# The last norm of a hybrid decoder step: sums by the constant matrix, statistics per token column, a 128-row correction operand, two blocks of 128 tokens

## The chip, the cores and the metric

The kernel runs on one core of a Trainium2 chip. The metric is the device time of one execution in microseconds (us), taken as the median of the runs; lower is better.

## The reference

The reference computes one inference step of a four-layer decoder for 1024 prompt tokens and 8 sample tokens, with a width of 2048. Two layers mix by pooling, two by windowed attention, and each layer ends in a norm over the width. Only the last norm matters here. For each token it is

```python
def layer_norm(x, g, b):
    mu = jnp.mean(xf, axis=-1, keepdims=True)
    var = jnp.mean(jnp.square(xf - mu), axis=-1, keepdims=True)
    return (xf - mu) * lax.rsqrt(var + LN_EPS) * g + b
```

applied to `ALPHA * x + sublayer(x)`, where the sublayer ends in a 2048 by 2048 product with `w_out_b`. The outputs `y_prompt` and `y_sample` are these normalised rows.

## The kernel before, in words

The tokens are worked in two chunks: chunk 0 has 512 tokens, chunk 1 has 520 (512 of the prompt and the 8 samples). Activations lie with the width across the 128 partitions: 16 groups of 128 channels, handled as 8 pairs p = 0 to 7, each a tile of 128 x 2 x T. All large products go as f32 split into a high and a low part, three passes each (lines 643, 644 and 645), and by a seven-product scheme over half chunks of 260 columns. `ACT` casts the high part of each weight block (L476) and `DVE` subtracts to get the low part (L491), some blocks ahead of the product. The order of the instructions of PE, DVE and ACT is that of the source: a helper, `in_order`, ties each instruction to the one before it on its engine. The queue of SP (DMA issue) and that of POOL have no such tie.

The change lies in `phase_end`, which runs the last three pairs (5, 6 and 7, called x, y and z there) of the last output product of chunk 1, and with them the norm of that chunk. A table `steps` says which small jobs go behind which of the 21 products of these three pairs (`TAIL`). The 520 columns have two halves: `Bh` (columns 260 to 519), whose statistics are made while products still run, and `A` (columns 0 to 259), whose statistics can only be made at the end. `less`, `rest`, `square` and `add` build the pre-norm value and the running sums of values and of squares. For half `Bh`, `sums` multiplies the running sums by a constant 128x128 matrix J with all elements 1/2048 (L1292), so that each of the 128 partitions gets the mean of each token; `stats` turns these into mean and reciprocal deviation on 128x260 tiles (L1299 to L1301 and the helper `rstd`, L859 to L862); `affine1` (DVE, L1310 and L1311) and `affine2` (ACT, L1318) apply them to a pair, and L1319 stores it.

Half `A` goes another way. `scale` (ACT, L1330) multiplies each pair by its gain. `turn` (L1413) transposes blocks of 128 tokens on PE, so that tokens come to lie across partitions, four channel groups to one PSUM bank of 128x512. There are three token blocks: 128, 128 and 4. `columns` (L1364) makes the sums of each token by 24 f32 products (two instructions each) that stream one column of J past a block of values, which gives one sum per partition. `moments` works on 128x3 tiles (L1374 to L1393), `lay` transposes the results into 6 rows (L1400, L1404), and `last_rows` (L1422) adds minus mean times gain and deviation times bias to each bank by one product with those 6 rows against 6 rows of gains and biases. `evict` multiplies the bank by the reciprocal deviation on its way to SBUF, on ACT for even banks (L1438), on DVE for odd ones (L1435), and each two banks are stored as 512 KB (L1436). The 6 rows of gains and biases are prepared by `rows0`, `rows1` and `rows2`: load, split, store to a scratch tensor in DRAM (L1344), and 12 small loads of one row each (L1351).

After the last product of the loop the source gives, in this order: the square and scale of the last piece, `affine1` of pair 1, the transposes of block 0 but for pair 7, `columns`, `affine1` of pair 2, the other transposes, `affine2` of pairs 1 and 2, `moments`, `affine1` of pair 3, `lay`, `last_rows`, the evictions of block 0, and then blocks 1 and 2 with the affine steps of pairs 3 and 4 between them.

PSUM banks come from rings: `psD` (3 banks), `psW` (4 banks) and `psO` (1 bank). SBUF slots (`mem.full`, `mem.half`) come from a list of 53, the one longest free first.

Of the kernel before, what the change touches and what calls it, by code (L numbers as in the profile page):

```python
# [16 lines left out]
P = 128  # L17
# [164 lines left out]
class Kern:  # L182
    def __init__(self, ctx, tc, io):
# [13 lines left out]
        self.gbs = one.tile([32, 2 * P], F32R, name="gbs")  # L197
        self.hcol = one.tile([P, 6], F32R, name="hcol")
        self.rows = one.tile([8, THM], F32R, name="rows")
# [1045 lines left out]
    def phase_end(self, c, xs, x_in, pre, acc, gc, bc, out):  # L1245
# [16 lines left out]
        BLK = (0, P), (P, 2 * P), (2 * P, TH)  # L1262
# [62 lines left out]
        def scale(p, js=(0, 1), away=False):  # L1325
            if p not in gx:
                gx[p] = self.pair_view(self.mem.full(), T) if away else tv(p)
            for j in js:
                m = gc + 2 * p + j
                nc.scalar.activation(gx[p][:, j, A], tv(p)[:, j, A], AF.Copy, scale=self.prm[:, m : m + 1])  # L1330

        def rows0():

            s = self.mem.half()
            raw, hi, lo = s.a[:32, :P], self.gbs[:32, :P], self.gbs[:32, P : 2 * P]
            nc.sync.dma_start(raw, io["gb"])
            box["f"] = s, raw, hi, lo

        def rows1():
            s, raw, hi, lo = box["f"]  # L1340
            nc.scalar.copy(hi, raw)
            nc.vector.tensor_sub(lo, raw, hi.bitcast(F32))
            s.free()
            nc.sync.dma_start(self.gbd[:], self.gbs[:32].bitcast(F32))  # L1344

        def rows2():
            for u in range(2):
                g = box["g", u] = self.mem.full()
                for k, (w, i) in enumerate(((0, 0), (0, 1), (0, 0), (1, 0), (1, 1), (1, 0))):
                    r = 16 * w + 8 * u  # L1350
                    nc.sync.dma_start(  # L1351
                        g.a[k : k + 1, :1024].rearrange("p (a b) -> p a b", a=8),
# [3 lines left out]
        def columns():  # L1356

            ps = box["c"] = self.psO()
            w = SPLIT[-1]
            for i, (a, z) in enumerate(((av, tv(w)), (qv, self.pair_view(q[w], T)))):  # L1360
                for b, (lo, hi) in enumerate(BLK):
                    srcs = [v[:, j, lo:hi] for v in (a, z) for j in range(2)]
                    for k, v in enumerate(srcs):
                        nc.tensor.matmul(  # L1364
                            ps[: hi - lo, 3 * i + b : 3 * i + b + 1], v, J[:, :1], start=k == 0, stop=k == 3
                        )

        def moments():

            ps = box["c"]  # L1370
            S = self.mem.half().a
            col = lambda i: S[:, 3 * i : 3 * i + 3]
            box["C"] = C = S[:, 32:50].rearrange("p (b k i) -> p b k i", b=3, k=2)
            nc.vector.memset(S[:, :6], 1.0)  # L1374
            full = ps[:, :6].rearrange("p (i b) -> p i b", i=2)
            to = S[:, :6].rearrange("p (i b) -> p i b", i=2)
            nc.vector.tensor_copy(to[:, :, :2], full[:, :, :2])
            e = BLK[2][1] - BLK[2][0]
            nc.vector.tensor_copy(to[:e, :, 2:], full[:e, :, 2:])
            m, v, qq, r, nm, sd = (col(i) for i in range(6))  # L1380
            box["r"] = r
            nc.vector.tensor_mul(qq, m, m)
            nc.vector.scalar_tensor_tensor(v, v, EPS, qq, op0=ALU.add, op1=ALU.subtract)
            nc.vector.tensor_scalar(nm, m, -1.0, None, op0=ALU.mult)
            self.rstd(v, r, qq)
            nc.vector.tensor_mul(sd, v, r)
            hi = self.hcol[:]
            nc.scalar.copy(hi, S[:, 12:18])
            h3 = hi.bitcast(F32).rearrange("p (k b) -> p b k", k=2)
            x3 = S[:, 12:18].rearrange("p (k b) -> p b k", k=2)  # L1390
            nc.vector.tensor_copy(C[:, :, :, 0], h3)
            nc.vector.tensor_copy(C[:, :, :, 1], h3)
            nc.vector.tensor_sub(C[:, :, :, 2], x3, h3)  # L1393

        def lay():

            ps = box["c"]
            for b, (lo, hi) in enumerate(BLK):
                n = hi - lo
                nc.tensor.transpose(  # L1400
                    ps[:6, P + lo : P + hi], box["C"][:n, b].rearrange("p k i -> p (k i)"),
                    self.cst[:n, K_ID : K_ID + n],
                )
            nc.scalar.copy(self.rows[:6, :TH], ps[:6, P : P + TH])  # L1404

        def turn(b, ps):
            lo, hi = BLK[b]
            for p in ps:
                for j in range(2):
                    i = 2 * p + j  # L1410
                    if i % 4 == 0 and (b, i // 4) not in X:
                        X[b, i // 4] = self.psW() if b != 1 or i >= 12 else self.psD()
                    nc.tensor.matmul(  # L1413
                        X[b, i // 4][: hi - lo, (i % 4) * P : (i % 4 + 1) * P], gx[p][:, j, lo:hi],
                        self.cst[:, K_ID : K_ID + P], is_transpose=True, start=i % 4 == 0, stop=False,
                        skip_group_check=True,
# [820 lines left out]
```

## Time and profile before

| | |
|---|---|
| median of 3 runs | 2376.43 us (2375.75 to 2378.41) |
| the profiled execution, its own time | 2374.82 us |
| its span, first to last instruction | 2373.1 us |
| busy in the span: DVE, ACT, POOL | 81%, 56%, 8% |
| mean granted TensorE clock | 0.996 |
| DMA traffic in the span | 669.20 MB, 282 GB/s |

The times in the timeline views are microseconds from the start of the span. A row of a timeline gives the start, the duration, the engine, the line of the kernel, the operation, the tile written and the tiles read, and in brackets the idle time of the engine just before with what ended it. PE is the matmul stream, PEld the weight loads that run beside it. DMA-issuing instructions stand under SPq. The last product of the loop ends about 26 us ahead of the end of the span, and everything that the change touches behind the loop lies in these 26 us.

### The profile page before, as it was taken

Reading aid. Unit: us, or ns where it says so; the run is one execution under the profiler, and the core shown is the slowest. Engines: PE = TensorE matmul, PEld = TensorE weight load, DVE = VectorE, ACT = ScalarE, POOL = GpSimd, SP = SyncE. Lnnn points to the kernel's source line nnn. Section 1 sums busy time; section 2 is a strip of 40 time slices with the busy share of each in tenths; the row PEclk is TensorE's granted clock in tenths of the full one; section 3 lists DMA queues with packets and bytes.
Section 4 is the critical chain, followed back from the end, with each engine's and each line's share of the span. In section 5 each row is a group of like instructions: output and inputs, shape, how many; then the busy total and the mean of one; then the engine's idle time right before and its main releaser. Section 6 shows DMA issues by size and latency. Waiting matters only on the chain. (4 is left out here: it accounts for less than half of the span.)

```text
span 2373.1 us, 46646 instructions
## 1 busy us (share of the span) xinstructions
PE 2342.9 (99%) x18497; PEld 2227.8 (94%) x18497; DVE 1913.2 (81%) x2372; ACT 1338.0 (56%) x2419; POOL 195.4 (8%) x369
## 2 busy tenths in 40 slices
PE   8999999999999999999999999999999999999999
PEld 6899999999999999998878899999999999999998
DVE  8787998776878868958987888887776768888786
ACT  4444446444446447644555656675666667546555
POOL 0111110010000000001111111100000000000000
PEclk9999999999999999999999999999999999999998
DMA  8668889889889988989888776788776668699784
GB/s 293 213 248 299 279 287 360 311 301 318 288 308 333 320 274 323 330 302 330 308 318 301 253 235 218 266 277 280 234 245 218 222 191 298 228 369 365 266 306 163
DMA packets 251932, 669.20 MB, mean 282 GB/s; under 512 B 25624, under 2 KB 106424, under 8 KB 251712
## 3 DMA queue, kind: packets, MB, share of 16 engines
q1 hardware_dynamic: 206240, 501.14, 62.9%
q0 software_dynamic: 45472, 165.07, 17.9%
q8 instruction: 145, 2.38, 0.4%
q14 instruction: 75, 0.61, 0.1%
HBM read 471.01 MB, written 185.59 MB: 277 GB/s over the span
## 5 line engine op out<-in xcount | busy, mean ns | idle before, releaser
L643 PE MATMUL pD<-m,m 128*128 128x260 f32 (+1 forms) x4752 | 1348.5, 284 | 10.1 <-ACT pD L584 4.5
L645 PE MATMUL pD<-m,m 128*128 128x260 f32 (+1 forms) x4752 | 1340.2, 282 | 3.1 <-DVE m L491 3.1
L644 PE MATMUL pD<-m,m 128*128 128x260 f32 (+1 forms) x4752 | 1339.5, 282 | 0.0
L643 PEld LDWEIGHTS pD<-m,m 128*128 128x128 f32 x4752 | 895.4, 188 | 22.3 <-issue 10.1
L645 PEld LDWEIGHTS pD<-m,m 128*128 128x128 f32 x4752 | 896.0, 189 | 4.5 <-DVE m L491 4.3
L491 DVE TENSOR_TENSOR m<-m,m 128x1024 fp32r<-128x1024 f32 x674 | 814.0, 1218 | 103.4 <-ACT m L476 62.0
L644 PEld LDWEIGHTS pD<-m,m 128*128 128x128 f32 x4752 | 895.6, 188 | 1.7 <-issue 1.4
L476 ACT CAST m<-m 128x1024 fp32r<-128x1024 f32 x674 | 701.4, 1048 | 303.2 <-DVE m L334 72.3
L671 PE MATMUL pD<-m,m 128*128 128x512 f32 x448 | 179.7, 401 | 8.1 <-ACT m L754 8.1
L672 PE MATMUL pD<-m,m 128*128 128x512 f32 x448 | 177.0, 395 | 1.2 <-DVE m L763 1.2
L673 PE MATMUL pD<-m,m 128*128 128x512 f32 x448 | 176.9, 395 | 0.0
L763 DVE TENSOR_TENSOR m<-m,m 128x1024 fp32r<-128x1024 f32 (+1 forms) x120 | 146.7, 1224 | 7.5 <-ACT m L754 6.0
L616 ACT COPY m<-pD 128x260 f32<-128x260 f32 (+1 forms) x83 | 31.1, 374 | 195.3 <-PE pD L645 194.9
L754 ACT CAST m<-m 128x1024 fp32r<-128x1024 f32 (+1 forms) x120 | 125.8, 1053 | 13.4 <-PE pD L672 5.2
L671 PEld LDWEIGHTS pD<-m,m 128*128 128x128 f32 x448 | 84.5, 189 | 30.1 <-ACT m L754 8.3
L334 DVE TENSOR_TENSOR m<-m,m 128x1024 f32<-128x1024 f32 x88 | 107.5, 1222 | 4.9 <-DMA m<-in_wia 2.4
L672 PEld LDWEIGHTS pD<-m,m 128*128 128x128 f32 x448 | 84.6, 189 | 21.0 <-DVE m L763 2.2
L604 DVE TENSOR_TENSOR m<-pD,m 128x260 f32<-128x260 f32 (+1 forms) x86 | 36.4, 424 | 83.7 <-PE pD L645 83.4
L673 PEld LDWEIGHTS pD<-m,m 128*128 128x128 f32 x448 | 84.5, 189 | 19.8
L1706 ACT ACTIVATE m<-m,sm 128x128 f32<-128x128 f32 x256 | 99.2, 390 | 0.0
L1027 PE MATMUL pD<-m,m 128*128 128x260 f32 (+1 forms) x528 | 91.5, 323 | 0.0
L1027 PEld LDWEIGHTS pD<-m,m 128*128 128x128 f32 x528 | 79.5, 188 | 8.2
(224 smaller groups left out, 2128.7 us busy)
## 6 DMA issues: line engine op xcount, KB each, us to landing
m<-in_wia SPq DMA_DIRECT2D x124, 512.0 KB
m<-in_wib SPq DMA_DIRECT2D x120, 512.0 KB
swia<-m POOLq DMA_DIRECT2D x64, 512.0 KB, 4.8
m<-swia SPq DMA_DIRECT2D x64, 512.0 KB
m<-swoa SPq DMA_DIRECT2D x64, 512.0 KB
swib<-m POOLq DMA_DIRECT2D x64, 512.0 KB, 5.3
m<-swib SPq DMA_DIRECT2D x64, 512.0 KB
m<-swob SPq DMA_DIRECT2D x56, 512.0 KB
```

What stands on the lines that cost most here:

```text
L334: self.nc.vector.tensor_add(s[out].a[:, :1024], s[x].a[:, :1024], s[y].a[:, :1024])
L476: self.nc.scalar.copy(hi.r[:, :1024], self.stream[self.cast].src().a[:, :1024])
L491: self.nc.vector.tensor_sub(lo.r[:, :1024], s.src().a[:, :1024], hi.a[:, :1024])
L643: nc.tensor.matmul(ps[:, :TH], wh[:, s], h, start=new and k == 0, stop=False, skip_group_check=on)
L644: nc.tensor.matmul(ps[:, :TH], wh[:, s], l, start=False, stop=False, skip_group_check=on)
L645: nc.tensor.matmul(ps[:, :TH], wl[:, s], h, start=False, stop=k == 7, skip_group_check=on)
L671: nc.tensor.matmul(ps[:], wh[:, s], h, start=par == 0 and k == 0, stop=False)
L672: nc.tensor.matmul(ps[:], wh[:, s], l, start=False, stop=False)
L673: nc.tensor.matmul(ps[:], wl[:, s], h, start=False, stop=par == 1 and k == 7)
L754: self.nc.scalar.copy(h.r[:, :n], s.a[:, :n])
L763: self.nc.vector.tensor_sub(l.r[:, :n], s.a[:, :n], h.a[:, :n])
L1027: nc.tensor.matmul(ps[:, : cs.stop - cs.start], ws[:, s], d[:, cs], start=f0 and k == 0, stop=l0 and k == 3,)
```

## The change

The sums of half `A` are made as those of half `Bh` are: by products with J into two banks (`sums_a`, 8 products of 128x260, in three portions). The statistics are made on 128x260 tiles. The correction operand gets 128 rows: minus the mean lies in rows 0 to 63, the deviation in rows 64 to 127, with the high part in rows 0 to 31 and 64 to 95 and the low part in the others; of the gains and biases only rows 0, 1, 32, 64, 65 and 96 are loaded, and the rest is zero, set by two 128x1024 memsets on POOL. The reciprocal deviation of a token, which the evictions need per partition, is had by transposing the statistics tile (`factors`, `factors2`). There are two token blocks of 128. The last 4 tokens of half `A` go apart: `spare` copies their 4 columns of each pair on POOL into a small tile ahead of `scale`, `scale` runs on 256 columns in place of 260, and `last_four` normalises them with four DVE operations on 128x64 and stores them to an output of their own. The scale of pair 6 moves from the step of the last product to behind it, the first 8 transposes move ahead of the sums, and the banks are taken from other rings.

```diff
-        self.gbs = one.tile([32, 2 * P], F32R, name="gbs")
-        self.hcol = one.tile([P, 6], F32R, name="hcol")
-        self.rows = one.tile([8, THM], F32R, name="rows")
...
-        BLK = (0, P), (P, 2 * P), (2 * P, TH)
+        A2 = slice(0, 2 * P)
+        four = self.small(NK * 4, 1)
+        f3 = four[:].rearrange("p (k t) -> p k t", k=NK)
...
-                nc.scalar.activation(gx[p][:, j, A], tv(p)[:, j, A], AF.Copy, scale=self.prm[:, m : m + 1])
+                nc.scalar.activation(gx[p][:, j, A2], tv(p)[:, j, A2], AF.Copy, scale=self.prm[:, m : m + 1])
+
+        def spare(p):
+            nc.gpsimd.tensor_copy(f3[:, 2 * p : 2 * p + 2, :], tv(p)[:, :, 2 * P : TH])
...
         def rows1():
-            s, raw, hi, lo = box["f"]
-            nc.scalar.copy(hi, raw)
-            nc.vector.tensor_sub(lo, raw, hi.bitcast(F32))
+            s, h = box["f"]
+            nc.scalar.copy(h.r[:32, :P], s.a[:32, :P])
+            nc.vector.tensor_sub(h.r[:32, P : 2 * P], s.a[:32, :P], h.a[:32, :P])
             s.free()
-            nc.sync.dma_start(self.gbd[:], self.gbs[:32].bitcast(F32))
+            nc.sync.dma_start(self.gbd[:], h.a[:32, : 2 * P])
+            h.free(True)
+            for u in range(2):
+                box["g", u] = self.mem.full()
+                nc.gpsimd.memset(box["g", u].a[:, :1024], 0.0)
 
         def rows2():
             for u in range(2):
-                g = box["g", u] = self.mem.full()
-                for k, (w, i) in enumerate(((0, 0), (0, 1), (0, 0), (1, 0), (1, 1), (1, 0))):
+                for k, w, i in ((0, 0, 0), (1, 0, 1), (32, 0, 0), (64, 1, 0), (65, 1, 1), (96, 1, 0)):
...
+        def sums_a(js):
+
+            z = SPLIT[-1]
+            if not js:
+                R[0] = self.psW(), self.psW()
+            for ps, a, w in zip(R[0], (av, qv), (tv(z), self.pair_view(q[z], T))):
+                for j in js or (0, 1):
                     nc.tensor.matmul(
+                        ps[:, :TH], J, (w if js else a)[:, j, A], start=not js and j == 0, stop=js == (1,),
                         skip_group_check=True,
                     )
 
+        def moments():
+
+            mb, vb = R[0]
+            w, h, S = self.mem.full(), self.mem.full(), [self.mem.half() for _ in range(4)]
+            m, v, qq, r = (t.a[:, :TH] for t in S)
+            X, M = w.a[:, : 2 * P], h.r[:, : 2 * P]
+            box["m"], box["r"], box["M"] = m, r, M
+            hi, lo = slice(0, 64), slice(64, P)
+            back32 = lambda k: nc.vector.tensor_sub(
+                M[k : k + 32], X[k : k + 32], h.a[k : k + 32, : 2 * P]
+            )
+            nc.scalar.copy(m, mb[:, :TH])
+            nc.vector.tensor_mul(qq, m, m)
+            nc.scalar.mul(X[hi], mb[hi, A2], -1.0)
+            nc.vector.scalar_tensor_tensor(v, vb[:, :TH], EPS, qq, op0=ALU.add, op1=ALU.subtract)
+            nc.scalar.activation(r, v, AF.Abs_reciprocal_sqrt)
+            nc.scalar.copy(M[hi], X[hi])
+            nc.vector.tensor_mul(qq, r, r)
+            nc.vector.scalar_tensor_tensor(qq, qq, -0.5, v, op0=ALU.mult, op1=ALU.mult)
+            nc.vector.scalar_tensor_tensor(r, qq, 1.5, r, op0=ALU.add, op1=ALU.mult)
+            nc.vector.tensor_mul(X[lo], v[lo, A2], r[lo, A2])
+            nc.scalar.copy(M[lo], X[lo])
+            back32(32)
+            back32(96)
+
+        def factors():
+
+            ps = box["c"]
+            for b in range(2):
+                nc.tensor.transpose(
+                    ps[:, b * P : (b + 1) * P], box["r"][:, b * P : (b + 1) * P], self.cst[:, K_ID : K_ID + P]
+                )
+
+        def factors2():
+            rc = box["rc"] = self.small(2, 1)
+            nc.scalar.copy(rc[:], box["c"][:, : 2 * P].rearrange("p (b t) -> p b t", b=2)[:, :, 0])
...
         def last_rows(b, ks):
-            lo, hi = BLK[b]
             for k in ks:
                 nc.tensor.matmul(
-                    X[b, k][: hi - lo], self.rows[:6, lo:hi], box["g", k // 2].r[:6, (k % 2) * 512 : (k % 2 + 1) * 512],
+                    X[b, k][:], box["M"][:, b * P : (b + 1) * P],
+                    box["g", k // 2].r[:, (k % 2) * 512 : (k % 2 + 1) * 512],
                     start=False, stop=True, skip_group_check=True,
                 )
...
+        def last_four():
+
+            wide = lambda a: a[:, None, 2 * P : TH].to_broadcast([P, NK, 4])
+            over = lambda i: self.prm[:, i : i + NK, None].to_broadcast([P, NK, 4])
+            nc.vector.tensor_sub(f3, f3, wide(box["m"]))
+            nc.vector.tensor_mul(f3, f3, wide(box["r"]))
+            nc.vector.tensor_mul(f3, f3, over(gc))
+            nc.vector.tensor_add(f3, f3, over(bc))
+            nc.sync.dma_start(io["y1c"], f3)
...
         square(z, A, 1)
+        spare(y)
+        spare(z)
         scale(z, (1,))
+        scale(y)
         affine1(1, Bh)
-        turn(0, range(z))
-        columns()
+        affine2(1, Bh)
+        X[0, 0], X[0, 1] = self.psD(), self.psD()
+        turn(0, 0, 8)
+        sums_a(())
+        sums_a((0,))
+        sums_a((1,))
+        X[0, 2], X[0, 3] = self.psW(), self.psW()
+        turn(0, 8, 16)
+        X[1, 0], X[1, 1] = self.psO(), self.psD()
+        turn(1, 0, 8)
         affine1(2, Bh)
-        turn(0, (z,))
-        turn(1, range(6))
-        affine2(1, Bh)
+        moments()
+        X[1, 2] = self.psW()
+        turn(1, 8, 12)
         affine2(2, Bh)
-        moments()
+        box["c"] = self.psW()
+        factors()
+        factors2()
         affine1(3, Bh)
-        lay()
         last_rows(0, range(4))
         last_rows(1, range(3))
         for k in range(4):
             evict(0, k)
-        turn(1, (6, 7))
+        last_four()
+        X[1, 3] = self.psD()
+        turn(1, 12, 16)
         last_rows(1, (3,))
-        turn(2, range(8))
-        last_rows(2, range(4))
+        affine2(3, Bh)
         affine1(4, Bh)
-        affine2(3, Bh)
         for k in range(4):
             evict(1, k)
         affine2(4, Bh)
-        for k in range(4):
-            evict(2, k)
```

In the table `steps`, `spare(p)` goes ahead of `scale(p)` for the pairs 0 to 5, and `scale(y)` leaves the last step.

More of the change, by code (lines that the diff above doesn't have):

```diff
@@ L1350, in rows2 @@
                     r = 16 * w + 8 * u
                     nc.sync.dma_start(
-                        g.a[k : k + 1, :1024].rearrange("p (a b) -> p a b", a=8),
+                        box["g", u].a[k : k + 1, :1024].rearrange("p (a b) -> p a b", a=8),
                         self.gbd[None, r : r + 8, i * P : (i + 1) * P],
                     )
[L1356 to L1393, printed above, removed]
@@ new lines, in factors, with turn @@
+        def factors():
[7 more added lines that the diff above has]
+            nc.scalar.copy(rc[:], box["c"][:, : 2 * P].rearrange("p (b t) -> p b t", b=2)[:, :, 0])
+        def turn(b, i0, i1):
+            for i in range(i0, i1):
+                p, j = divmod(i, 2)
+                nc.tensor.matmul(
+                    X[b, i // 4][:, (i % 4) * P : (i % 4 + 1) * P], gx[p][:, j, b * P : (b + 1) * P],
+                    self.cst[:, K_ID : K_ID + P], is_transpose=True, start=i % 4 == 0, stop=False,
+                    skip_group_check=True,
+                )
```

60 lines of the change are left out of this document (23 added, 37 removed).

## The prediction

> **What bounds the kernel now.** I read the page's busy shares first, then the PE timeline of the end, then the ACT, DVE and SP timelines beside it, and last the table by stretches for the granted clock and the DMA rate.
>
> ```profile
> PE 2342.9 (99%) x18497; PEld 2227.8 (94%) x18497; DVE 1913.2 (81%) x2372; ACT 1338.0 (56%) x2419; POOL 195.4 (8%) x369
> ```
>
> PE is busy 99% of the span, so what runs beside the products costs nothing unless it holds PE, and all that is exposed is the stretch behind the last product. Here is that stretch on PE, with an earlier row (L1292) for comparison:
>
> ```profile
> 2329.52 3.67 PE L1292 MATMUL pD<-m,cst 128*128 128x260 f32 x16
> ...
> 2347.46 1.04 PE L1413 MATMUL pD<-cst,m 128*128 128x128 f32 x8
> ...
> 2351.01 5.25 PE L1364 MATMUL pO<-cst,m 128*128 128x1 f32 x48
> 2356.19 3.25 PE L1413 MATMUL pD<-cst,m 128*128 128x128 f32 x14
> ...
> 2360.41 3.35 PE L1422 MATMUL pD<-m,rows 6*128 6x512 f32 x7 [0.45 <-ACT rows L1404]
> ...
> 2368.25 1.09 PE L1422 MATMUL pD<-m,rows 6*4 6x512 f32 x4
> ```
>
> The loop's products end at 2347.46. The one-column sums take 5.25 us; the correction products can begin at 2360.41, once the rows are made. Around them ACT and DVE work so:
>
> ```profile
> 2345.03 1.10 ACT L1318 ACTIVATE m<-m,prm 128x260 f32<-128x260 f32 x2 [2.74 <-DVE m L1311]
> ...
> 2349.18 0.40 ACT L1279 ACTIVATE m<-m 128x260 f32<-128x260 f32 x1
> 2349.49 1.30 ACT L1330 ACTIVATE m<-m,prm 128x260 f32<-128x260 f32 x3
> 2350.70 0.40 ACT L1279 ACTIVATE m<-m 128x260 f32<-128x260 f32 x1
> 2351.01 0.49 ACT L1330 ACTIVATE m<-m,prm 128x260 f32<-128x260 f32 x1
> 2351.41 2.07 ACT L1318 ACTIVATE m<-m,prm 128x260 f32<-128x260 f32 x4
> ```
>
> ```profile
> 2347.54 0.69 DVE L1283 TENSOR_TENSOR m<-m,m 128x520 f32<-128x520 f32 x1
> ...
> 2358.40 0.69 DVE L1310 TENSOR_TENSOR m<-m,m 128x520 f32<-128x520 f32 x1
> 2359.13 0.70 DVE L1311 TENSOR_TENSOR m<-m,m 128x520 f32<-128x520 f32 x1
> 2361.67 1.60 DVE L1435 TENSOR_SCALAR m<-pD,m 128x512 f32<-128x512 f32 x2 [1.84 <-PE pD L1422]
> ...
> 2368.91 1.40 DVE L1435 TENSOR_SCALAR m<-pD,m 4x512 f32<-4x512 f32 x2 [2.59 <-PE pD L1422]
> ```
>
> ACT has no gap from 2345.03 to 2353.5. The first odd eviction starts at 2361.67, the last, of the 4-token block, ends at 2370.31. What the stores do, and the clock:
>
> ```profile
> 2362.48 1.20 SPq L1436 DMA_DIRECT2D out_y1a<-m  x2
> ...
> 2369.71 0.92 SPq L1436 DMA_DIRECT2D out_y1a<-m  x2
> ```
>
> ```profile
> 2351.00:2353.80 2.80, 2.80 (x32) 2.75 (x31) 0.27 (x2) 2.48 (x6) 0.00 (x0) 1.00 0.13 46
> 2353.80:2367.40 13.60, 13.15 (x58) 9.81 (x58) 7.10 (x20) 5.26 (x11) 0.00 (x0) 0.50 0.40 149
> ...
> 2363.30:2370.50 7.20, 6.04 (x27) 2.92 (x25) 4.08 (x6) 3.85 (x7) 0.00 (x0) 0.71 0.96 367
> 2370.50:2371.80 1.30, 0.00 (x0) 0.00 (x0) 0.00 (x0) 0.00 (x0) 0.00 (x0) 0.64 0.11 24
> 2371.80:2373.10 1.30, 0.00 (x0) 0.00 (x0) 0.00 (x0) 0.00 (x0) 0.00 (x0) 0.50 0.00 0
> ```
>
> The last three columns are granted clock, DMA share, GB/s. Two things stand here. The clock falls to half at 2353.80, amid one-column sums. And from 2363.30 on, 0.8 us behind the first store's issue, the DMA engines are 96% busy for 7.2 us: four stores of 512 KB and two of 260 KB drain back to back. So the end is set by a chain (sums, statistics, rows, first evictions) that starts this drain, by the drain, and by a tail: 1.3 us of the tiny store of 4 tokens, 1.3 us of waits.
>
> **The change part by part.** *Sums.* The 48 one-column instructions go; 8 products of 128x260 come, each two instructions as the 16 of L1292 were for 8: 3.67 us. First run 8 transposes (1.04 us, to 2348.50); the running sums are ready, since the last `add` ends at 2348.23. At full clock the sums end at 2348.50 + 3.67 = 2352.17, with the result some 0.15 us later (a row of 0.38 issued every 0.23). The pieces that they wait for come earlier: ACT does square and scale of the last piece before the scale of pair 6, so the second square starts two scales (0.81 us) earlier, at 2349.9. The means are done half a us ahead of the deviations' sums, at 2351.87.
>
> *What is late next is ACT.* It has to scale as before and does `affine2` of pair 1 (half of the 2.07 us from 2351.41) ahead of the statistics: free at 2352.4. The statistics start there, 2352.40, not when PE is done. The shorter scales (256 of 260 columns) gain under 0.05 us; I count nothing.
>
> *Statistics.* They have been seen on this tile size in the loop:
>
> ```profile
> 2331.47 0.38 ACT L1299 COPY m<-pD 128x260 f32<-128x260 f32 x1 [0.42 <-PE pD L1292]
> ...
> 2333.69 0.42 ACT L859 ACTIVATE m<-m 128x260 f32<-128x260 f32 x1 [1.84 <-DVE m L1301]
> ```
>
> ```profile
> 2331.88 0.43 DVE L1300 TENSOR_TENSOR m<-m 128x260 f32<-128x260 f32 x1 [0.51 <-ACT m L1299]
> ...
> 2334.14 0.43 DVE L860 TENSOR_TENSOR m<-m 128x260 f32<-128x260 f32 x1 [0.49 <-ACT m L859]
> 2334.60 0.43 DVE L861 SCALAR_TENSOR_TENSOR m<-m 128x260 f32<-128x260 f32 x1
> ```
>
> From L1299 to L1300 is 0.41, from one dependent DVE row to the next 0.46, across ACT's root 0.45. In order: mean copy 0.42, square 0.46, variance 0.47, root 0.46, three steps of refinement 1.38, deviation 0.46, ACT's cast 0.42, low part 0.42: 4.49 us, so the operand stands at 2356.89. The products need it then: 2356.93 for 2360.41, **3.48 us earlier**.
>
> *Reciprocal deviation per token.* Its two transposes come at 2355.6, where PE waits anyway; ACT then has the cast and `affine2` of pair 2 (1.03) ahead of the 0.2 us copy: 2357.6. It isn't last.
>
> *Correction products.* 8 of 128x512 for 12; the 128 rows have no row of their own, and I take 0.48 each at half clock, as 7 in 3.35 with 6 rows (the bounds are 0 and double that, 3.8 us for the eight). Before, the first odd eviction began 1.26 us behind the first of them; DVE's `affine1` of pair 3 (2358.40 to 2359.83, 1.35 to the next start) fits inside that, as it ends at 2358.2. So it begins at 2358.19, and the first store is issued at 2359.0 for 2362.48: again 3.48.
>
> *Clock.* The falling clock is no loss in my sum: dense sums hold it at 1.00 through the statistics' start at least, and later transposes have slack: 2352.2 + 20 of 0.13 is 2354.8, and the next needed is at 2355.6. The Trainium skill ("TensorE: Matmul & The Clock Gate", Part 4) says that transposes don't count as busy for the clock; by that the clock may be half for all 20. In the trace 14 transposes at half clock (3.25 us) didn't raise it, which agrees. Those 20 would then end at 2352.2 + 20 x 0.23 = 2356.8, the two small ones at 2357.3, and the operand's products start 0.4 us later: 3.1 in place of 3.5.
>
> *Drain and tail.* The same four and two large stores: 7.2 us. The 4 tokens now make one store of 32 KB inside the drain, in pieces of 256 bytes: between 0.1 us (by the rate of 367 GB/s) and 1.3 (as the tiny store took); I take 0.2, since the pieces spread over 128 rows. The tail of 1.3 us goes. Drain 2359.8 to 2367.2 or, with its later stores ready at 2362.75 and 2363.5, no gap over 0.2; then 1.3 us: the span ends at 2368.7, 2373.1 - 2368.7 = 4.4.
>
> *Work on POOL and SP.* POOL was idle here. Its prices bracket the new ones:
>
> ```profile
> L1685 POOL MEMSET m<- 128x256 f32 x16 | 5.2, 323 | 51.7 <-PE pO L1747 29.7 <-PE pD L644 8.8 <-DMA th<-m 7.8
> ...
> L962 POOL MEMSET m<- 128x15 f32 x16 | 1.8, 116 | 30.2 <-PE pD L644 9.0 <-DVE m L724 7.8 <-DMA g<-m 5.6
> ```
>
> ```profile
> 2322.62 7.83 SPq L1351 DMA_DIRECT2D m<-gbd  x12
> ```
>
> Two memsets of 1024 columns are some 1.1 us each (323 ns and 0.86 ns for each column over 256), behind the loop's step at about 2317, done before the row loads issue at 2322.62: hidden. The 8 copies of 128x8 cost 0.1 to 0.3 us each on POOL; ACT's `scale` may wait for them, but the copied values stand a step earlier. DVE could be held. The Trainium skill ("SBUF — State Buffer", the section on two separate sides) has DVE operations with two SBUF inputs and POOL operations that read SBUF exclude each other; no row of before shows it. By it, three copies ahead of 2345.03, where DVE feeds ACT, would cost up to 1 us together. In my sum DVE loses 0 to 1 us to POOL, and I take 0.1, near nothing, as POOL's work is short. **Sum: 4.3 us earlier**, 2374.82 - 4.3 = 2370.5 for the profiled execution. That execution lies 1.6 us under the median; the forecast is given on the median: 2376.43 - 4.3 = **2372.1 us**. Gain or loss under 0.2% (4.75 us, 2371.7 to 2381.2) is what a measurement can't tell from no change, so the forecast lies just inside "same".
>
> **The rivals.** *The end follows the evictions.* If the drain isn't the bound, the last DVE eviction counts: 2358.2, then two evictions, the four small operations, `affine1`, two evictions (4 x 0.77 + 0.8 + 1.35) give 2363.4 against 2370.31, 6.9 us: 2369.5. For it: the 512 KB stores come from two buffers that are ready early. Against: 96% DMA share.
>
> *The chain slips.* If PE runs at half clock through the sums (7.3 us), or the copies hold DVE a full us, the statistics begin 1 to 3 us later: the sums at half clock end at 2355.8 for 2352.4, so 1 us of gain is left. 2373.4 to 2375.4. Against: PE has no gap that would halve the clock ahead of them. That the change doesn't do what it says, no shorter sums, ends here too.
>
> *Slower: the queue behind the row loads.* The twelve loads on SP now wait for POOL's memsets, and behind them in SP's queue are the reloads of pairs 2 to 4 and the last weight block, whose cast and subtraction are
>
> ```profile
> 2337.33 1.05 ACT L476 CAST m<-m 128x1024 fp32r<-128x1024 f32 x1 [1.60 <-DMA m<-in_wob]
> ```
>
> ```profile
> 2340.61 1.22 DVE L491 TENSOR_TENSOR m<-m,m 128x1024 fp32r<-128x1024 f32 x1
> ```
>
> The cast ends at 2338.3, DVE wants it at 2340.61: 2.3 us to spare. If memsets come d us late, all that follows is d - 2.3 late; from d = 6.6 the gain of 4.3 is gone, from 11.4 the kernel is slower by 0.2%: 2381. For it: a memset waits for the last reader of its slot, perhaps a matmul. Against: slots freed longest are taken first, and the row loads took the same kind of slot before.
>
> **How the numbers follow.** Forecast 0.58 (2371.0 to 2373.2, a third of it past 0.2%), evictions 0.15, slipping chain 0.16, slower 0.11. Faster: 0.19 + 0.15 = 0.34; same: 0.39 + 0.16 = 0.55; slower 0.11. The range runs from the evictions' 2369.5 to the slipped chain's 2375.4 with some tenths for the runs' spread, and leaves out the slower case: 2369.3 to 2375.8. The unknown costs (products of 128 rows up to 3.8 us, small store 1.3, DVE 1.0) lie inside it alone, not all together.
>
> **What would show it.** Sums of 16 instructions in 3.7 us at clock 1.00; ACT's mean copy right behind an affine step near 2352.4; the first correction product near 2356.9; the first 512 KB store at 2359.0; DMA share over 0.9 for 7 us; no tiny tail. A gap in the products before 2347, a long wait ahead of the row loads, or a first store later than 2360 would prove it wrong.

## The result, and the profile after

| | before | after |
|---|---|---|
| median of 22 runs | 2375.80 us (2373.52 to 2378.41) | 2371.84 us (2369.46 to 2374.10) |
| ratio, 95% interval | | 0.9984 (0.9978 to 0.9991) |
| the profiled execution: its span | 2373.1 us | 2369.8 us |

The medians lie 3.96 us apart; by the ratio the kernel got 0.16% faster. The interval leaves out 1, so a gain under 0.2%, which the prediction took for too small to be told from no change, could be told. The forecast was 2372.1 us: 4.3 us off the median shown then, 2376.43 us. From the median of the 22 runs the same 4.3 us lead to 2371.5 us, so that the forecast time lies within 0.3 us of the measured one is in part luck.

Both spans contain a loop of 2347 us whose length varies by a few us between executions. The first transpose behind the loop stands at 2345.69 to 2350.05 in four profiles of the kernel before and its variants, at 2346.53 to 2349.84 in nine of the changed kernel and its variants, and in the two compared here at 2347.46 and at 2348.03, the later one in the faster kernel. So everything below is measured from that first transpose, and the *tail* is the time from there to the end of the span: 25.60 us before, 21.82 after, 3.78 less. (The prediction and the expectations have 25.64 and 21.77, from spans rounded to 0.1 us.) Whether the loop itself changed by some tenths is not shown. Here is PE in the tail after the change (start, duration, engine, line, operation, tiles):

```profile
2348.03 1.04 PE L1412 MATMUL pD<-cst,m 128*128 128x128 f32 x8
2348.90 3.67 PE L1367 MATMUL pD<-m,cst 128*128 128x260 f32 x16
2352.41 1.04 PE L1412 MATMUL pD<-cst,m 128*128 128x128 f32 x8
2353.28 0.60 PE L1412 MATMUL pO<-cst,m 128*128 128x128 f32 x4
2353.72 1.04 PE L1412 MATMUL pD<-cst,m 128*128 128x128 f32 x8
2356.29 0.44 PE L1401 MATMUL pD<-cst,m 128*128 128x128 f32 x2 [1.53 <-DVE m L1391]
2357.69 1.72 PE L1420 MATMUL pD<-m,m 128*128 128x512 f32 x4 [0.96 <-DVE m L1380]
```

The sums (L1367) take 3.67 us in 16 instructions, right behind 8 transposes. PE is then early: it stands still for 1.53 us for the reciprocal deviation and for 0.96 us for the operand. The same stretch on ACT and on DVE:

```profile
2352.04 1.09 ACT L1317 ACTIVATE m<-m,prm 128x260 f32<-128x260 f32 x2
2353.03 0.36 ACT L1383 COPY m<-pD 128x260 f32<-128x260 f32 x1
```

```profile
2356.72 0.87 DVE L1380 TENSOR_TENSOR m<-m,m 32x256 fp32r<-32x256 f32 x2
2357.62 0.70 DVE L1309 TENSOR_TENSOR m<-m,m 128x520 f32<-128x520 f32 x1
2358.35 0.70 DVE L1310 TENSOR_TENSOR m<-m,m 128x520 f32<-128x520 f32 x1
2358.97 1.41 DVE L1432 TENSOR_SCALAR m<-pD,sm 128x512 f32<-128x512 f32 x2
...
2362.55 1.40 DVE L1432 TENSOR_SCALAR m<-pD,sm 128x512 f32<-128x512 f32 x2
```

ACT copies the mean (L1383) directly behind the affine step (L1317), without a gap: ACT is late, not PE. DVE has no gap either from the operand's low parts (L1380) over the affine step of pair 3 to the first two odd evictions (L1432). The last two evictions end at 2363.95, 5.9 us ahead of the end. The stores, and the table by stretches (the last three columns are granted clock, DMA share, GB/s):

```profile
2359.78 1.00 SPq L1433 DMA_DIRECT2D out_y1a<-m  x2
2361.35 0.33 SPq L1447 DMA_DIRECT2D out_y1c<-sm  x1
2361.80 0.84 SPq L1318 DMA_DIRECT2D out_y<-m  x1
2363.37 1.12 SPq L1433 DMA_DIRECT2D out_y1a<-m  x2
2364.59 0.43 SPq L1318 DMA_DIRECT2D out_y<-m  x1
```

```profile
2348.90:2352.60 3.70, 3.70 (x20) 3.18 (x19) 2.96 (x6) 3.70 (x11) 0.59 (x1) 1.00 0.21 72
2360.60:2368.20 7.60, 1.22 (x6) 0.87 (x4) 3.25 (x7) 2.35 (x5) 0.00 (x0) 0.72 0.93 351
2360.60:2367.60 7.00, 1.22 (x6) 0.87 (x4) 3.25 (x7) 2.35 (x5) 0.00 (x0) 0.74 0.99 378
2367.70:2369.80 2.10, 0.00 (x0) 0.00 (x0) 0.00 (x0) 0.00 (x0) 0.00 (x0) 0.50 0.02 5
2368.30:2369.80 1.50, 0.00 (x0) 0.00 (x0) 0.00 (x0) 0.00 (x0) 0.00 (x0) 0.50 0.00 0
```

The sums run at full clock. From 0.8 us behind the first store's issue the DMA engines are 93% busy for 7.6 us, then 1.5 us pass with no data. Nearly all of the data is through after 7.0 us (99% busy), 2.2 us ahead of the end. Counted from the first transpose:

| us behind the first transpose | before | predicted | after |
|---|---|---|---|
| mean's copy on ACT | | 4.94 | 5.00 |
| first correction product | 12.95 | 9.47 | 9.66 |
| first 512 KB store issued | 15.02 | 11.54 | 11.75 |
| end of the span | 25.60 | 21.3 | 21.82 |

So 3.27 us were won up to the first store, and 0.51 behind it (10.58 before, 10.07 after).

Of the 3.29 us at the first correction product, the shorter sums are the smaller part. The sums start at 0.87 in place of 3.55 (2.68 us won): before the change they stood behind 14 transposes, which waited 0.42 and 0.57 us for ACT's scales. The sums take 3.67 in place of 5.25 (1.58 won). Then the mean waits 0.46 us for ACT, and from its copy to the first correction product there are 4.66 us, where it was 4.15 from the end of the one-column sums (0.46 and 0.51 lost). No run moved the one-column sums ahead of those transposes, so how much the old sums would have gained from the order alone is not shown.

### The profile page after: what moved, and what is told of

Same layout as the page of the kernel before. It is cut to its first block, busy times and chain, and to the rows that moved or that the text cites. A ratio compares the mean times of both kernels' runs of the same rounds, so it can differ in the third digit from the quotient of the medians.

```text
span 2369.8 us, 46551 instructions
## 1 busy us (share of the span) xinstructions
PE 2335.5 (99%) x18444; PEld 2224.0 (94%) x18444; DVE 1914.7 (81%) x2369; ACT 1338.8 (56%) x2420; POOL 203.1 (9%) x379
## 5 line engine op out<-in xcount | busy, mean ns | idle before, releaser
L751 ACT CAST m<-m 128x1024 fp32r<-128x1024 f32 (+1 forms) x120 | 125.8, 1052 | 13.6 <-PE pD L669 5.2
```

The source lines that it names most:

```text
L751: self.nc.scalar.copy(h.r[:, :n], s.a[:, :n])
```

## The experiments

Theory: the chain of sums, statistics and operand sets when the stores start; their drain and a wait follow. Main rival: the end follows the last evictions. Unless said otherwise a number is taken from one profile and counted from the first transpose.

**1. Before, without the third block.** `turn(2, ...)`, `last_rows(2, ...)` and `evict(2, ...)` are taken out.

```diff
-        turn(2, range(8))
-        last_rows(2, range(4))
...
-        for k in range(4):
-            evict(2, k)
```

> The kernel before, leaving out the block of 4 tokens (its transposes, products, evictions and two small stores; those 4 rows of the output are not written). The measure is the tail: from the first transpose behind the loop to the end of the span, 25.64 us in the kernel before (2347.46 to 2373.1). Theory (the end is set by the start of the stores, their drain of 7.2 us and a fixed wait; the third block only adds its tiny stores at the end): the tail gets about 1.3 us shorter, 24.3. Rival (the end follows the last eviction): the last eviction moves from 2370.3 to 2366.3, so the tail gets about 4 us shorter, 21.6, and the whole gain of the change would be the third block's.

```profile
2349.23 6.39 PE L1364 MATMUL pO<-cst,m 128*128 128x1 f32 x48
...
2359.78 3.35 PE L1422 MATMUL pD<-m,rows 6*128 6x512 f32 x7 [0.46 <-ACT rows L1404]
```

The tail was 26.17 us, *longer*, and neither theory has that: its one-column sums took 6.39 us where the first profile of before has 5.25, for the same 48 instructions, and so the first store came 1.14 us later (16.16 for 15.02). Run 10 takes this up. Behind the first store there were 10.01 us for 10.58: the third block costs 0.57 us there. By the rival it would have been 4. The theory's size, 1.3, was too large.

**2. After, without the last 4 tokens.** The copies on POOL, the four DVE operations and the 32 KB store are left out.

```diff
-            nc.gpsimd.tensor_copy(f3[:, 2 * p : 2 * p + 2, :], tv(p)[:, :, 2 * P : TH])
+            pass
...
-        last_four()
```

> The changed kernel, leaving out the last 4 tokens of half A altogether (the copies on POOL, the four DVE operations, the 32 KB store; that output is not written). Tail of the changed kernel: 21.77 us (2348.03 to 2369.8). Theory (drain): 32 KB less to drain and nothing else on the path, 0.1 to 0.3 us shorter, 21.5. Rival (evictions): the four operations of 0.22 us stand ahead of an affine step and the last two evictions on DVE, so the end comes 0.9 us earlier, 20.9.

```profile
2361.26 1.40 DVE L1432 TENSOR_SCALAR m<-pD,sm 128x512 f32<-128x512 f32 x2
```

The tail was 21.71. The last eviction ended 0.92 us earlier (15.00 for 15.92) and the end came 0.1 us earlier: in the changed kernel the evictions don't set the end. The theory holds, and taking 4 tokens apart costs next to nothing.

**3. After, with two stores of 260 KB fewer.**

```diff
-            nc.sync.dma_start(out[:, 2 * p : 2 * p + 2, :], t)
+            if p not in (3, 4):
+                nc.sync.dma_start(out[:, 2 * p : 2 * p + 2, :], t)
```

> The changed kernel, leaving out two of the stores of 260 KB (pairs 3 and 4 of half Bh; their arithmetic stays, these parts of the output are not written). Theory (drain): the drain gets shorter until the last store's own readiness sets it: issued at 2364.2 in the changed kernel, so data to 2366.9 and the end near 2368.3, 1.5 us earlier: tail 20.3. Rival (evictions): nothing that the evictions wait for is gone, tail 21.8 as before the edit.

```profile
2364.10:2364.60 0.50, 0.00 (x0) 0.00 (x0) 0.50 (x1) 0.34 (x1) 0.00 (x0) 0.50 0.01 1
2364.90:2367.30 2.40, 0.00 (x0) 0.00 (x0) 0.00 (x0) 0.00 (x0) 0.00 (x0) 0.50 1.00 399
2367.70:2370.00 2.30, 0.00 (x0) 0.00 (x0) 0.00 (x0) 0.00 (x0) 0.00 (x0) 0.50 0.01 4
```

The tail was 21.36: 0.46 shorter, between the two, and nearer to the rival. The last store was issued at 15.99, as expected, but the end came 5.4 us behind that issue, where I had reckoned with 4.1. The rows show why the drain is no bound here: with the two stores gone it ran empty (DMA share 0.01 from 2364.10) before the last two stores were ready, as the theory said. Their data was then nearly all through at 2367.7, 2.4 us ahead of the end, for 2.2 in the changed kernel. How long the wait behind the last data is isn't constant, and why stays open. The tail of this run doesn't tell the theories apart. Nor does it exclude that the end simply follows the last store's issue: in the changed kernel the end comes 5.3 us behind it. Run 2 speaks against that, as its last store was issued 0.7 us earlier (15.86 for 16.56) and the end came 0.1 us earlier.

**4. After, with the sums made twice.**

```diff
+        both = R[0]
+        for js in (), (0,), (1,):
+            for ps, a, w in zip(both, (av, qv), (tv(SPLIT[-1]), self.pair_view(q[SPLIT[-1]], T))):
+                for j in js or (0, 1):
+                    nc.tensor.matmul(
+                        ps[:, :TH], J, (w if js else a)[:, j, A], start=not js and j == 0, stop=js == (1,),
...
```

> The changed kernel with the 8 products of the sums made twice over into the same banks, 3.67 us more on PE. Theory (the chain sums, statistics, operand sets the start of the drain, with 0.7 us of slack on PE as ACT is late): everything behind moves by about 2.9 us, tail 24.7, the mean's copy on ACT now directly behind the products. Rival (ACT's scales and affine steps hide the sums, so that their length doesn't matter): tail 21.8 to 22.3.

ACT in this run:

```profile
2352.80 1.08 ACT L1317 ACTIVATE m<-m,prm 128x260 f32<-128x260 f32 x2
2356.44 0.38 ACT L1383 COPY m<-pD 128x260 f32<-128x260 f32 x1 [2.56 <-PE pD L1521]
```

Now the mean's copy waits 2.56 us for the products, the first correction product stands at 12.32 (2.66 later) and the tail is 24.54 (2.72 longer). The added products hold PE for 3.51 us, from their first start to that of the next transposes. So the chain goes through to the end, and PE had about 0.9 us to spare.

**5. After, with 6 rows in the correction products.**

```diff
-                    X[b, k][:], box["M"][:, b * P : (b + 1) * P],
-                    box["g", k // 2].r[:, (k % 2) * 512 : (k % 2 + 1) * 512],
+                    X[b, k][:], box["M"][:6, b * P : (b + 1) * P],
+                    box["g", k // 2].r[:6, (k % 2) * 512 : (k % 2 + 1) * 512],
```

> The changed kernel with the correction products taken over 6 rows of the operand in place of 128 (timing only: four of the six parts of the correction are left out of the sum). Theory (a product of 512 columns costs the same with 6 rows as with 128, and the drain sets the end): the 8 products stay 0.43 us apart at half clock, the first store 11.75 us behind the first transpose, tail 21.8. As to the clock: if rows that carry nothing count for the granted clock, it comes back to 1.00 within the products as in the changed kernel; if only filled rows count, it stays at 0.50 to the end of the products. Rival (128 rows cost time): the products come closer and the first store earlier, by up to 0.5 us.

```profile
2357.88 1.36 PE L1420 MATMUL pD<-m,m 6*128 6x512 f32 x4
...
2359.47 1.05 PE L1420 MATMUL pD<-m,m 6*128 6x512 f32 x2
```

The first product came 1 us earlier, since the 6 rows need no low part, but the first store stood at 11.74 and the tail at 21.79, as in the changed kernel: DVE's affine step stands ahead of the first odd eviction, and the products aren't on the path. Two products at half clock take 1.05 us, as in the changed kernel with 128 rows (0.43 apart): the rows cost no time. For the clock, look at two stretches each of this run and, below, of the changed kernel, the first from the fall of the clock to its next step. (In these profiles the clock stays at half for 3.4 us or a whole multiple of it: 13.6 us in the kernel before, 17.0 in run 10.)

```profile
2358.80:2362.10 3.30, 3.30 (x10) 1.79 (x8) 3.17 (x8) 3.27 (x8) 0.00 (x0) 0.50 0.32 114
2362.20:2365.50 3.30, 0.09 (x1) 0.00 (x0) 2.91 (x6) 1.85 (x4) 0.00 (x0) 0.50 0.99 370
```

```profile
2358.10:2361.40 3.30, 3.30 (x12) 2.62 (x10) 3.16 (x9) 3.26 (x8) 0.00 (x0) 0.50 0.48 178
2361.50:2364.90 3.40, 0.32 (x2) 0.00 (x0) 2.42 (x4) 1.45 (x3) 0.00 (x0) 1.00 1.00 375
```

PE is busy for the whole first stretch in both. With 128 rows the clock is back at 1.00 in the next, with 6 rows it isn't; in runs 6 and 8, with 128 rows, it came back in the same way. Most of the 128 rows of gains hold zeros, and they count all the same.

**6. After, with the statistics ahead of an affine step on ACT.**

```diff
             nc.scalar.copy(M[hi], X[hi])
+            affine2(1, Bh)
...
-        affine2(1, Bh)
         X[0, 0], X[0, 1] = self.psD(), self.psD()
```

> The changed kernel with the affine step of pair 1 on ACT moved from ahead of the statistics into ACT's gap of 1.6 us within them. Theory (ACT is late, and the chain from the statistics to the first store sets the end): the mean's copy starts when its products are done, 4.3 us behind the first transpose in place of 5.0, and everything behind it moves by 0.7: first correction product 8.95, first store 11.05, tail 21.1. Rival (the end hangs on the affine steps and evictions on ACT and DVE, whose work is the same): tail 21.6 to 21.8.

```profile
2353.48 0.38 ACT L1383 COPY m<-pD 128x260 f32<-128x260 f32 x1
```

The mean's copy started at 4.14, the first correction product at 8.81, the first store was issued at 10.90, and the tail was 21.07: 0.75 us off the tail by one moved line, as ACT's lateness said. The rival is out for this kernel, as far as one run tells: the unchanged order up to the first store gave tails of 21.71 to 22.11 (the changed kernel, runs 2, 5 and 8).

**7. After, for an early drain, each bank stored alone.** Besides the edit of run 6: the affine step of pair 2 lies in the statistics' gaps too, half of pair 3's ahead of them on DVE, the evictions go ahead of other steps, and

```diff
             if k % 2:
...
-                nc.sync.dma_start(
-                    io["y1a"][b * P : (b + 1) * P, (k - 1) * 512 : (k + 1) * 512], Y[b, k // 2].a[:, :1024]
+            nc.sync.dma_start(io["y1a"][b * P : (b + 1) * P, k * 512 : (k + 1) * 512], y)
```

> The changed kernel, arranged for an early and short drain: the affine steps of pairs 1 and 2 on ACT lie in the gaps of the statistics, half of that of pair 3 on DVE lies ahead of them, evictions go ahead of the other affine steps, and each bank is stored by itself (256 KB) as soon as it is evicted. Theory (start of the drain plus bytes left plus a fixed wait): the statistics start 0.7 us earlier, the first store is issued at 10.3 us behind the first transpose in place of 11.75, and 260 KB less are left to drain then (0.7 us): tail 19.5, some 2.3 us under the changed kernel; the time near 2369.5 us, 0.27% under the kernel before. Rival (evictions): the last eviction moves only by the 0.7 us of the statistics and the waits between: tail 21.0.

```profile
2357.26 1.80 SPq L1447 DMA_DIRECT2D out_y1a<-m  x4
```

```profile
2358.10:2366.30 8.20, 1.41 (x6) 0.90 (x4) 3.54 (x9) 2.83 (x6) 0.00 (x0) 0.50 0.97 326
2358.10:2365.60 7.50, 1.41 (x6) 0.90 (x4) 3.54 (x9) 2.83 (x6) 0.00 (x0) 0.50 1.04 347
```

The first store came at 10.10 (10.3 expected), 1.65 us earlier, but the tail was 21.03 for the 19.5 expected, as the rival has it (run 9 tells the two apart): the time behind the first store grew from 10.07 to 10.93. The DMA engines were 97% busy at 326 GB/s for 8.2 us, where the changed kernel had 351 GB/s at 93%; while they are fully busy (share 1.04 and 0.99) it is 347 GB/s for 378. With pieces of 2 KB the same bytes drain more slowly. My 260 KB less was a mistake as well, as that store lay ahead of the drain already. Of 11 runs the median was 2371.25 us, 0.9983 (0.9974 to 0.9992) of before: no better than the changed kernel.

**8. After, with each copy on POOL four times.**

```diff
-            nc.gpsimd.tensor_copy(f3[:, 2 * p : 2 * p + 2, :], tv(p)[:, :, 2 * P : TH])
+            for _ in range(4):
+                nc.gpsimd.tensor_copy(f3[:, 2 * p : 2 * p + 2, :], tv(p)[:, :, 2 * P : TH])
```

> The changed kernel with each of the 8 copies on POOL made four times. In the changed kernel DVE's stretch from its eviction L611 of pair 5 to that of pair 6 (no idle time in it, three copies beside it) takes 8.81 us, as long as before the change (8.82). Rule that DVE and POOL exclude each other, with DVE as the loser: twelve copies of 0.26 us would hold DVE for up to 3 us in that stretch. Theory (POOL is the loser; DVE's work isn't held): the stretch stays 8.8 us, POOL's copies take 0.6 to 1.1 us each, and the tail stays 21.8, as nothing waits for the copies.

POOL and, at the two ends of the stretch, DVE:

```profile
2339.07 7.72 POOL L1333 COPY sm<-m 128x8 f32<-128x8 f32 x12 [8.90 <-DVE m L611]
```

```profile
2338.58 0.43 DVE L611 TENSOR_TENSOR m<-pD,m 128x260 f32<-128x260 f32 x1 [0.58 <-PE pD L642]
...
2347.40 0.42 DVE L611 TENSOR_TENSOR m<-pD,m 128x260 f32<-128x260 f32 x1
```

DVE's stretch took 8.82 us with twelve copies beside it, to the hundredth what it took with none. The twelve took 7.72 us, 0.64 each, against 0.19 for the shortest copy of this run. Here POOL lost time and DVE didn't. The tail was 22.11, 0.3 longer, all of it behind the first store (11.74), where one run can't say more.

**9. The arrangement of run 7 with 512 KB stores.**

As run 7, but the store is that of the changed kernel, and the evictions of the second block keep their order, with `last_four` ahead of them. The other edits, which both runs have, in the statistics and in the order behind them:

```diff
+            affine1a(3, Bh)
...
+            affine2(1, Bh, (0,))
...
+            affine2(1, Bh, (1,))
+            affine2(2, Bh)
...
-        affine2(1, Bh)
...
-        affine2(2, Bh)
...
-        affine1(3, Bh)
+        affine1b(3, Bh)
...
-        last_four()
+        affine2(3, Bh)
```

> The arrangement of e7_after_drain_early, but each two banks stored together (512 KB, pieces of 4 KB) as in the changed kernel. Theory (drain whose rate hangs on the size of the pieces: 7.6 us with 4 KB, 8.25 us with 2 KB for the same bytes): the first store is issued at 10.5 us behind the first transpose (11.75 in the changed kernel), the drain takes 7.6 us again, tail 20.5; the time near 2370.5. Rival (the drain was longer in e7 for another reason, the evictions or the order of the stores): tail 21.0 as in e7.

```profile
2357.80:2364.80 7.00, 0.08 (x1) 0.00 (x0) 3.21 (x8) 2.50 (x5) 0.00 (x0) 0.67 0.99 378
```

First store at 10.44, tail 20.71, median of 9 runs 2369.84 us: 0.9976 (0.9966 to 0.9986) of before. The tail lies between the theory's 20.5 and the rival's 21.0, and as the order of the evictions differs from run 7 too, the 0.32 us between the two tails needn't be those of the pieces alone. The last eviction on DVE ends at 14.61 in both runs, so it doesn't explain them. What shows the pieces' part is the rate with the DMA engines fully busy: 378 GB/s here and in the changed kernel, 347 in run 7. This version beats the kernel before by 0.24%, and its tail is 1.11 us shorter than that of the changed kernel. The two intervals overlap, so that it also beats the changed kernel rests on the profiles.

**10. Before, once more.** No edit.

> The kernel before, unchanged, for another phase of the clock. In its first profile the granted clock fell to half 6.33 us behind the first transpose, and the first correction product stood at 12.95; in e1_before_no_third, with the same chain, 4.71 and 14.09. Theory (the falling clock amid the one-column sums is part of the length of this chain): the first correction product stands between 12 and 14.5, the later the earlier the clock falls, by about 0.7 us for each us. Rival (the difference of 1.14 us in e1 came from its edit): 12.95 within 0.1, wherever the clock falls.

```profile
2353.60 5.90 PE L1364 MATMUL pO<-cst,m 128*128 128x1 f32 x48
2359.44 3.25 PE L1413 MATMUL pD<-cst,m 128*128 128x128 f32 x14
...
2363.66 3.35 PE L1422 MATMUL pD<-m,rows 6*128 6x512 f32 x7 [0.45 <-ACT rows L1404]
```

```profile
2350.05:2355.20 5.15, 4.00 (x32) 3.15 (x30) 3.75 (x8) 5.15 (x14) 0.00 (x0) 1.00 0.23 78
2355.30:2372.30 17.00, 16.55 (x80) 12.31 (x80) 7.11 (x20) 6.04 (x13) 0.00 (x0) 0.50 0.44 165
```

The clock fell at 5.24 here, and the first correction product stood at 13.61, between the other two as the theory said: falls at 4.71, 5.24 and 6.33 go with 14.09, 13.61 and 12.95. The same program's tail was 27.03 us for 25.60, of which 0.66 lie ahead of the first store and the rest behind it. The length of this chain hangs on where the clock falls; in the changed kernel and in runs 2, 3, 5 and 8, which keep its order up to the first store, that store stands at 11.74 or 11.75 wherever the clock falls (9.48 to 15.55). What a fall earlier than 9.4 would do to the changed kernel no run shows.

**11. Before, with the second block's transposes behind the correction products.**

```diff
-        turn(1, range(6))
         affine2(1, Bh)
...
         last_rows(0, range(4))
+        turn(1, range(6))
         last_rows(1, range(3))
```

> The kernel before with the 12 transposes of the second block moved from behind the sums to behind the first block's correction products. In the kernel before PE does these transposes (2356.2 to 2359.4, at half clock) while the statistics on 128x3 tiles are done at 2358.4, so the transposes of the rows wait 0.8 us for PE. Theory: the first correction product comes 0.8 us earlier where the clock falls at the same place, about 12.1, and the tail gets shorter by as much, as the drain starts earlier. So this part of the gain (3.3 us at the first correction product) is one of order, not of the sums. Rival (the statistics are the longer way): 12.9 as before.

```profile
2369.30:2370.30 1.00, 1.00 (x5) 0.67 (x5) 0.34 (x1) 0.98 (x2) 0.00 (x0) 0.50 0.00 0
```

The clock fell at 3.96, earlier than in any other run, so absolute places can't be compared. From the end of the one-column sums to the first correction product it was 3.43 us, for 4.15 in the kernel before and 4.16 in runs 1 and 10: 0.7 us are a matter of order, as said. The tail was not shorter but 29.89 us: the moved transposes and the products behind them ran at half clock, the third 512 KB store was issued 4.8 us behind the first (2.9 before), and the drain stood empty (the row shows 1 us of it). A drain is the bound only while the work ahead of it keeps it fed.

## Why the prediction was right, point by point

*Sums.* Right: 3.67 us at clock 1.00, and PE ready ahead of ACT. The prediction had half a us of slack, run 4 about 0.9. That most of the gain comes from where the sums start, and not from their length, the prediction doesn't say, though its sum has it.

*ACT is late next.* Right: copy at 5.00 for 4.94, without a gap behind the affine step. Run 6 moved that step, and the tail got 0.75 us shorter.

*Statistics.* Right in kind, 0.13 us too short: 4.66 us from the mean's copy to the first product for 4.53 (4.49 of rows and 0.04 to the product). With the 0.06 of ACT and 0.02 behind the product this makes 3.27 us for 3.48 up to the first store.

*First store.* Its place was right to 0.21 us. Which engine holds it was only half right: the prediction had the first odd eviction 1.26 us behind the first product, with DVE's affine step inside that. Run 5 shows that DVE alone holds it, as the products could come 1 us earlier for nothing.

*Clock.* Right that the fall is no loss after the change: runs 2, 3, 5 and 8 and the changed kernel had it between 9.48 and 15.55, with the first store at 11.74 or 11.75 in each. What the prediction took from one profile as a fixed length, the chain before, is one draw: 12.95 was the shortest of the runs. Against the tail of run 10, 27.03, the changed kernel's would be 5.21 us shorter, so that the sum came so close to the profile it was worked out from is in part luck. The other way that the prediction gives, half clock through the 20 transposes, did not come: they ran at 1.00 (8 in 1.04 us). Its reading of the 14 transposes at half clock was hasty as well: counted in steps of 3.4 us from the fall at 2353.80, they lie across two steps, with one-column sums in the first and 0.45 us of idle PE in the second. In run 10 the clock came back to 1.00 behind a step filled by 16 transposes (of the block of 4 tokens) and the start of one product:

```profile
2369.00:2372.40 3.40, 3.40 (x17) 1.77 (x16) 0.57 (x1) 0.15 (x1) 0.00 (x0) 0.50 1.02 389
2372.50:2375.80 3.30, 0.85 (x4) 0.16 (x2) 1.40 (x2) 1.25 (x2) 0.00 (x0) 1.00 0.30 97
```

So the rule that the prediction quotes there, by which transposes don't count for the clock, does not hold in this case.

*Drain and tail.* The mechanism was right (runs 2, 6), the size off. Of the forecast 4.3 us, 0.8 were to be won behind the first store (1.3 for the tiny store, less 0.2 for the new one, 0.2 for a gap and 0.1 for DVE), and 0.51 were. With the 0.21 lost up to the first store this is why 4.3 became 3.78. The mis-sized term is the wait of 1.3 us behind the data. Behind the tiny stores it is that short, but behind the large ones it is 2.2 us in the changed kernel and 2.4 in run 1, where the tiny stores are left out:

```profile
2362.50:2369.40 6.90, 2.40 (x7) 1.00 (x5) 2.86 (x5) 2.77 (x6) 0.00 (x0) 0.50 0.98 376
2369.50:2371.80 2.30, 0.00 (x0) 0.00 (x0) 0.00 (x0) 0.00 (x0) 0.00 (x0) 0.50 0.02 7
```

So a large part of the tiny stores' 1.3 us lay in a wait that is there without them. What makes up this wait is open. The rival's view fits the kernel before better than I gave it: there the end came 2.8 us behind the last eviction of the third block in the profile and in runs 10 and 11, though run 1 puts only 0.57 us on that block.

*POOL and SP.* The memsets took 0.96 us each for the 1.1 estimated (323 ns and 0.86 ns for each of the 768 columns more are 0.98, so the 1.1 was a slip), and were done before the row loads were issued:

```profile
2314.62 0.96 POOL L1349 MEMSET m<- 128x1024 f32 x1 [25.14 <-PE pD L642]
2316.05 0.95 POOL L1349 MEMSET m<- 128x1024 f32 x1 [0.48 <-PE pD L642]
```

The copies are longer than thought (0.26 to 1.13 us for 0.1 to 0.3), and DVE lost nothing for the 0.1 set down. The Trainium skill ("SBUF — State Buffer", the section on two separate sides) has a DVE operation with two SBUF inputs and a POOL operation that reads SBUF exclude each other, with the one that starts first as the holder; the copies' 0.64 for 0.19 us beside busy DVE agree, but no run shows DVE held.

*Rivals.* The slipping chain and the queue behind the row loads did not happen: the loads were issued at 2322.92, for 2322.62 before.

## What to carry to other kernels

At the end of a kernel, find what starts the last drain of stores and how long that drain is, and work on the start of it; an instruction that stands in source order ahead of the one that the chain needs, as the affine step on ACT did, costs up to its length (moved away, 0.86 us of its 1.09 at the mean's copy). Smaller pieces bring the first store forward, but their lower rate can cost more than that. And a time taken from one profile of a stretch in which the clock falls is one draw from a range: take a second profile before building a sum on it.

## What the runs showed of the hardware that was not expected

- One-column products neither hold the clock nor bring it back while PE counts as fully busy. In four profiles with these sums the clock fell to half amid them, 3.96 to 6.33 us behind the first transpose, and the 48 instructions took 7.08, 6.39, 5.90 and 5.25 us, the longer the earlier it fell. The first row is the stretch ahead of the fall in the kernel before, 31 of its 33 instructions one-column ones. The second is the one behind the fall in run 11, one-column products alone, at half clock to its end and on:

```profile
2350.38:2353.80 3.42, 3.29 (x33) 3.05 (x33) 0.86 (x3) 3.10 (x8) 0.00 (x0) 1.00 0.11 38
```

```profile
2352.80:2356.20 3.40, 3.40 (x24) 3.35 (x23) 0.00 (x0) 2.04 (x5) 0.00 (x0) 0.50 0.35 121
```

- The fall itself needn't be theirs: in run 11 only the last 0.4 us of the 3.4 ahead of it held one-column products, and PE was idle for 1.1 us of it.
- Products over 6 rows did not bring the clock back in 3.3 us of full PE time (run 5, and likewise from 2360.6 to 2364.0 in the kernel before); over 128 rows, mostly zeros on one side, they did in three (the changed kernel, runs 6 and 8). Sixteen transposes did too (run 10).
- With the DMA engines fully busy, stores with 2 KB pieces drained at 347 GB/s, with 4 KB pieces at 378.
